# RWKV-7 recurrence of a two-layer decoder trunk: both halves of the inverse in one buffer, the first half ended in the fixed order, gate products and late norms at other places

## The chip, the cores and the metric

The kernel runs on one core of a Trainium2 chip, as one launch. The metric is the device time of that launch in microseconds; the median of three runs stands for the kernel.

## What is computed

The trunk has two layers over 512 positions of width 1024, in float32. Layer 0 is a sparse attention with an indexer, layer 1 is an RWKV-7 time mixing; each is followed by an MLP with squared ReLU. The change touches layer 1 alone:

```python
def step(state, inp):
    r_t, w_t, k_t, v_t, kk_t, b_t = inp
    sa = jnp.einsum('bhvk,bhk->bhv', state, -kk_t)
    state = state * w_t + sa[..., None] * b_t + v_t[..., None] * k_t
    return state, jnp.einsum('bhvk,bhk->bhv', state, r_t)
...
y = (y - mean) * rsqrt(var + LNX_EPS) * lnx_w + lnx_b     # per head of 64
out = (y + bonus) * g                                     # g = sigmoid(xg @ g1) @ g2
return out @ w_o
```

There are 16 heads of 64 columns.

## The kernel before

The 512 steps of the recurrence are done in eight chunks of 64 steps (`NCH` = 8). Within a chunk the dependence of a step on the earlier ones is a unit triangular 64 by 64 system for each head and chunk. Its inverse is built from two 32 by 32 diagonal blocks, inverted on VectorE (`solve`, 30 steps of one multiply, line 1025, and one addition, line 1026), and a corner joined from them by TensorE (`merge1`, line 1120, and `merge2`, line 1132). The inverse comes in two halves: the first is for chunks 0 to 3, the second for chunks 4 to 7. Each half is gathered through DRAM into a tile `tn` of its own, solved in place, copied in a transposed form (`tt`, line 1029, the other half of the same tile), written back to DRAM (`dm` and `dt`, lines 1032 and 1034) and read again into `T11` and `Mt` (lines 1039 and 1042). `tn` and most other large tiles come from one pool of 21 buffers with the tag `b8` (`NB8`); tiles of 512 columns come from one of 17 (tag `t`).

`invert` is a generator. `run(t)` takes steps from it until their estimated cost exceeds `t` nanoseconds; `yield HOLD` ends a call. It is called after each of the eight blocks of the value projection (lines 1205 to 1207) with `RUNW`, and at several places of the recurrence with `RUN1` and `RUN2`.

Up to the value projection a planner sets the order of the instructions from priorities and estimated costs. What follows stands in a `manual_schedule` block: there the five engines' queues take the instructions in the order of the source, while work that was emitted earlier may still be placed between them. In that block each chunk n goes through `step_z` (line 1266, copied by line 1268), `step_u` (line 1274, copied by line 1278), `step_n` (the next state, lines 1292 and 1296), `step_y` (line 1316) and the operands of the next chunk, `opn`/`opl` (lines 1177, 1178, 1172) and `opt` (line 1189). `vcopy` (line 1217) takes the eight value blocks from PSUM into the two tiles `VT`; `vmean` (line 1251) and `vload` (line 1258, GpSimd) prepare them. `g2` makes the gate, eight products of four matmuls (lines 1235 to 1238), of which the last needs a conversion on ScalarE (line 1416). The norm of chunk n's result is `gA` (square, ScalarE), `gB` (sums, VectorE, line 1335), `gC` (root, ScalarE), `gD` (VectorE lines 1347 to 1352, then GpSimd lines 1357 to 1360), and `turn` transposes it (line 1369). `out(f)` makes the operands of the output projection for half f of the positions, one of eight column groups for each `pull` (line 1377, then a split into a high and a low part by line 104 on ScalarE and line 101 or 99). `wom(f, m)` is one output product of 24 matmuls (lines 119 to 121) and a residual addition (line 1393); its weights are converted by ScalarE (line 93) and split by VectorE (line 101) in `wload`, ahead of use.

Of the kernel before, what the change touches and what calls it, by code (L numbers as in the profile page):

```python
# [7 lines left out]
F32 = mybir.dt.float32  # L8
# [757 lines left out]
def rwkv(c, x, ks, gi):  # L766
# [232 lines left out]
    def invert():  # L999
        dn, dm = (c.dram.tile([2, 2, 2, 32, 32, 32], F32, name=v) for v in ("dn", "dm"))  # L1000
        dt = c.dram.tile([2, 2, 32, 32, 32], F32, name="dt")
        mt = [t.rearrange("p q n t -> p (q n) t") for t in Mt]
        for q in range(2):
            qs = slice(16 * q, 16 * q + 16)
            for f in range(2):
                for e in range(2):
                    for b in range(2):
                        r = slice(e * 64 + b * 32, e * 64 + b * 32 + 32)
                        nc.sync.dma_start(dn[f, e, b, qs].rearrange("h i j -> i h j"),
                                          mt[f][r, qs, b * 32:b * 32 + 32])  # L1010
            yield HOLD
        tn = [c.b8("tn", F32, (128, 2, 32, 32)) for _ in range(2)]
        for f in range(2):
            nc.sync.dma_start(tn[f][:, 0].rearrange("p i j -> p (i j)"), dn[f].rearrange("e b h i j -> (e b h) (i j)"))
        yield HOLD
        for f in range(2):
            yield from solve(f, tn[f][:, 0], tn[f][:, 1], mt[f], dm[f], dt[f])

    def solve(f, tn, tt, mt, dm, dt):
        pr = c.t("pr")  # L1020
        for k in range(30, 0, -1):
            nr = 31 - k
            sh = [128, k, nr]
            pv = pr[:, :k * nr].rearrange("p (a b) -> p a b", a=k)
            nc.vector.tensor_mul(pv, tn[:, 0:k, k:k + 1].to_broadcast(sh), tn[:, k:k + 1, k + 1:].to_broadcast(sh))  # L1025
            nc.vector.tensor_add(tn[:, 0:k, k + 1:], tn[:, 0:k, k + 1:], pv)
            yield 2 * (k * nr * 1.04 + 157)
        nc.vector.memset(tn.rearrange("p i j -> p (i j)")[:, 0:1024:33], 1.0)
        nc.vector.tensor_copy(tt, tn.rearrange("p i j -> p j i"))
        stage.append(f)  # L1030
        yield HOLD
        nc.sync.dma_start(dm.rearrange("e b h i j -> (e b h) (i j)"), tn.rearrange("p i j -> p (i j)"))
        for e in range(2):
            nc.sync.dma_start(dt[e].rearrange("h i j -> h (i j)"), tt[e * 64:e * 64 + 32].rearrange("p i j -> p (i j)"))
        yield HOLD
        T11[f] = [c.t("T11").rearrange("p (h j) -> p h j", j=32) for _ in range(2)]
        for e in range(2):
            for g in range(2):
                nc.sync.dma_start(T11[f][g][e * 64:e * 64 + 32], dt[e, g * 16:(g + 1) * 16].rearrange("h i j -> i h j"))
            for b in range(2):  # L1040
                r = slice(e * 64 + b * 32, e * 64 + b * 32 + 32)
                nc.sync.dma_start(mt[r, :, b * 32:b * 32 + 32], dm[e, b].rearrange("h i j -> i h j"))
        yield HOLD

    def run(t):
        while t > 0:
            d = next(inv, None)
            if d is None:
                break
            t -= d  # L1050
# [134 lines left out]
    @c.site("opt")  # L1185
    def opt(n, te=TE):
        pt = c.bank2((128, 8, 2, 64))
        for q in range(8):
            nc.tensor.transpose(pt[:, q].rearrange("p e i -> p (e i)"), sl(KB, n, q).rearrange("p a b -> p (a b)"), ident)
        nc.scalar.activation(BL[n][:, 0, :, 64:128], pt[:, :, 0], AF.Copy)  # L1190
        for i in range(2):
            cp(te[i], BL[n][E2[1 - i], 1, :, 64:128], pt[E2[i], :, 1])
# [38 lines left out]
    @c.site("g2")  # L1231
    def g2(m):
        ms = slice(m * 128, (m + 1) * 128)
        p = c.bank("g")
        nc.tensor.matmul(p, ah[:, ms], sg[0], start=True, stop=False)
        nc.tensor.matmul(p, ah[:, ms], sg[1], start=False, stop=False)
        nc.tensor.matmul(p, al_[:, ms], sg[0], start=False, stop=False)
        nc.tensor.matmul(p, bh[0:96, ms], sg[2][0:96], start=False, stop=True)
        gT[m] = c.t("gT")
        nc.scalar.activation(gT[m], p, AF.Copy, scale=0.5)  # L1240
# [13 lines left out]
    @c.site("vload")  # L1254
    def vload(n):
        SV[n] = sv[:, n % 2]
        for e in range(2):
            nc.gpsimd.tensor_tensor(SV[n][E2[1 - e], e], vt(n)[:, :, e],
                                    vm[E2[n % 2], n // 2, e::2, None].to_broadcast([64, 8, 64]), op=OP.add)

    @c.site("step_z")
    def step_z(n):
        pz = c.bank("g", (128, 8, 64))
        for q in range(8):
            for e in range(2):
                nc.tensor.matmul(pz[E2[e], q], AL[n][:, q, e], SV[n][:, e, q], start=True, stop=True)
        for e in range(2):
            nc.scalar.activation(Zb[E2[e], :, e], pz[E2[e]], AF.Copy)
# [133 lines left out]
    with c.tc.manual_schedule(engines=set(MAN)):  # L1402
        while not stage:
            run(1)
        until(0)
        for i in VL[:3]:
            vcopy(i)
        vmean(0)
        vload(0)
        opn(1, 0)  # L1410
        for i in VL[3:]:
            vcopy(i)
        del ps
        opn(1, 1)
        (ah, al_), (bh, bl) = ((a.rearrange("p a b -> p (a b)") for a in c.wget(0)) for _ in range(2))
        nc.scalar.activation(bh[64:96], bl[64:96].bitcast(F32), AF.Copy)
        g2(0)
        g2(1)
        opt(1, (0, 0))
        g2(2)  # L1420
        g2(3)
        step_z(0)
        for m in range(4, 8):
            g2(m)
        vload(1)
        run(RUN1)
        merge2(0, merge1(0))
        for n in range(NCH - 1):
            more = True
            if n:  # L1430
                step_z(n)
            if n % 2 and more:
                vmean((n + 1) // 2)
            if n == 1:
                lnw = g3(c.t("lnw"))
                nc.sync.dma_start(lnw, c.aps["lnw"])
            if n and more:
                acopy(n + 1)
                opn(n + 1, 0)
                vload(n + 1)  # L1440
            for k in GB.get(n, ()):
                gB(k)
            if n < 3:
                run(RUN2)
            step_u(n)
            if more and n != 3:
                sa[n + 1] = merge1(n + 1)
            for k in GB.get(n, ()):
                gC(k)
            if more:  # L1450
                pn = step_s(n)
                step_n(n, pn)
            py = step_r(n)
            if more:
                sbd(n)
            step_y(n, py)
            for k in GB.get(n, ()):
                gD(k)
            if n < 2:
                run(RUN2)  # L1460
            elif n == 2:
                until(1)
            if n and more:
                opn(n + 1, 1)
            if n == 3:
                sa[4] = merge1(4)
            if more:
                merge2(n + 1, sa[n + 1])
            if n and n < NCH - 2:
                opt(n + 1, (0, 0) if n < 3 else TE)  # L1470
            for k in TU.get(n, ()):
                turn(k)
            for k in GA.get(n, ()):
                gA(k)
            if n == PF1:
                c.wdma()
        n = NCH - 1
        step_z(n)
        c.prefetch(1)
        w0 = out(0)  # L1480
        pull(w0, 4)
        step_u(n)
        gB(5)
        gC(5)
        py = step_r(n)
        step_y(n, py)
        turn(4)
        gA(6)
        gB(6)
        gC(6)  # L1490
        gD(5)
        pull(w0, 4)
        gD(6)
        gA(7)
        gB(7)
        gC(7)
        gD(7, nc.vector)
        xo.extend(c.b8("x") for _ in range(2))
        for i in range(2):
            nc.sync.dma_start(xo[i].rearrange("p a b -> p (a b)"), xs[i])  # L1500
        w1 = out(1)
        for m in range(KC):
            wom(0, m)
            if m in TM:
                turn(TM[m])
            if m > 5:
                pull(w1, 3)
    pull(w1, 8)
    mi = MlpIn(c, gi)
    for m in wo(1):  # L1510
# [7 lines left out]
MAN = (mybir.EngineType.PE, mybir.EngineType.Activation, mybir.EngineType.DVE, mybir.EngineType.SP, mybir.EngineType.Pool)  # L1518
GA = {2: (0,), 3: (1, 2), 4: (3,), 5: (4,), 6: (5,), 7: (6,)}
GB = {3: (0,), 4: (1, 2), 5: (3,), 6: (4,), 7: (5,)}  # L1520
TU = {4: (0,), 5: (1, 2), 6: (3,)}
TM = {1: 5, 3: 6, 5: 7}
PF1 = 5
RQ = 3
VP = (6, 7, 8)
# [1 line left out]
WA = 4  # L1527
LP = 2
OP2 = 1
RUNW = 5000  # L1530
RUN1 = 9000
RUN2 = 2500
XG = 2
# [126 lines left out]
```

## Time and profile before

| | us |
|---|---|
| median of three runs | 1394.31 (1394.28 to 1398.93) |
| the profiled execution, its own time | 1400.04 |
| span of its records | 1398.3 |
| TensorE busy | 1305.3 (93%) |
| VectorE busy | 801.1 (57%) |
| ScalarE busy | 601.8 (43%) |
| GpSimd busy | 176.7 (13%) |

Times within the profile are microseconds from the start of the span. In a timeline row the first number is the start, the second the duration of the instruction or of the merged run of them, then engine, line, operation, output and inputs, and in brackets how long the engine had stood idle and what released it. TensorE's busy time counts a matmul until its modelled end, so a busy stretch is not one at the full clock; the granted clock is given beside it as a share of 2.4 GHz.

### The profile page before, as it was taken

The page shows a single profiled execution, that of the slowest core. Times are in us where ns is not written, and L with a number is a line of the kernel's source. Part 1 is how long each engine was busy: PE and PEld are TensorE (multiplying, and loading weights), DVE is VectorE, ACT ScalarE, POOL GpSimd, SP SyncE. Part 2 cuts the span into 40 slices and gives each one's busy share as a digit, 9 for nine tenths or more (in the row PEclk, how much of TensorE's full clock was granted, in tenths as well). Part 3 has the DMA queues.
Part 4 walks back from the last instruction along what each step waited for, and adds up shares of the span by engine and source line. Part 5 has one row for each costly group of instructions (what it writes and reads, how often), then busy time and mean ns, then how long its engine had stood idle before and what let it go on. Part 6 is the DMA issues. An engine that isn't in the chain of part 4 may idle for free.

```text
span 1398.3 us, 20066 instructions
## 1 busy us (share of the span) xinstructions
PE 1305.3 (93%) x8197; PEld 1070.6 (77%) x8197; DVE 801.1 (57%) x1407; ACT 601.8 (43%) x1024; POOL 176.7 (13%) x176
## 2 busy tenths in 40 slices
PE   8989899999999999999998968884999999999997
PEld 6766566888888888898677856763888888888887
DVE  5689974454421545259889886566565433244523
ACT  5535693343311434139765425653444331134421
POOL 0385750000000000000000011354020000000000
PEclk9999999999999999999999988996999999999999
DMA  7100023221323215232203421414432132321401
GB/s 282 61 30 31 1 75 109 97 90 61 120 95 117 90 60 181 91 106 76 90 31 87 140 53 40 78 26 165 133 109 82 69 121 90 121 90 62 170 10 61
DMA packets 63932, 125.95 MB, mean 90 GB/s; under 512 B 32608, under 2 KB 35296, under 8 KB 63072
## 3 DMA queue, kind: packets, MB, share of 16 engines
q1 hardware_dynamic: 61600, 122.44, 26.6%
q10 hardware_dynamic: 2240, 2.24, 0.5%
q8 instruction: 64, 1.05, 0.3%
q14 instruction: 28, 0.23, 0.1%
HBM read 115.74 MB, written 6.82 MB: 88 GB/s over the span
## 4 chain that ended last, share of the span: by engine, by line
PE 80%; DVE 12%; ACT 4%; issue 2%; POOL 1%; DMA 0%; DVEq 0%; ACTq 0%; SPq 0%; POOLq 0%
PE g L121 19%; PE g L119 19%; PE g L120 19%; PE g L628 2%; DVE rot L411 1%; PE d L613 1%; DVE w L101 1%; DVE acc L497 1%; DVE L L587 1%; DVE m L495 1%; PE g L993 1%; DVE pr L1025 1%; PE g L1274 1%; PE g L1292 1%; PE d L386 1%
## 5 line engine op out<-in xcount | busy, mean ns | idle before, releaser
L101 DVE TENSOR_TENSOR w<-wraw,w 128x1024 fp32r<-128x1024 f32 x189 | 229.7, 1239 | 116.4 <-ACT w L93 116.2
L93 ACT ACTIVATE w<-wraw 128x1024 fp32r<-128x1024 f32 x198 | 201.0, 1048 | 135.3 <-DMA wraw<-in_wblk 103.6
L119 PE MATMUL g<-sh,w 128*128 128x512 f32 (+1 forms) x608 | 216.5, 356 | 0.0
L120 PE MATMUL g<-sl,w 128*128 128x512 f32 (+1 forms) x608 | 216.2, 356 | 0.0
L121 PE MATMUL g<-sh,w 128*128 128x512 f32 (+1 forms) x608 | 216.2, 356 | 0.0
L120 PE MATMUL g<-al,w 128*128 128x512 f32 x512 | 199.3, 389 | 0.6 <-DVE al L257 0.6
L119 PE MATMUL g<-ah,w 128*128 128x512 f32 x512 | 199.7, 390 | 0.0
L121 PE MATMUL g<-ah,w 128*128 128x512 f32 x512 | 199.4, 389 | 0.3 <-DVE w L101 0.3
L273 ACT ACTIVATE sh<-r 128x512 fp32r<-128x512 f32 x64 | 40.4, 631 | 227.0 <-DVE r L271 227.0
L119 PEld LDWEIGHTS g<-sh,w 128*128 128x128 f32 x608 | 114.9, 189 | 16.4
L120 PEld LDWEIGHTS g<-sl,w 128*128 128x128 f32 x608 | 114.9, 189 | 16.2
L121 PEld LDWEIGHTS g<-sh,w 128*128 128x128 f32 x608 | 114.9, 189 | 16.2
L120 PEld LDWEIGHTS g<-al,w 128*128 128x128 f32 x512 | 96.1, 188 | 20.8 <-DVE al L257 1.0
L121 PEld LDWEIGHTS g<-ah,w 128*128 128x128 f32 x512 | 96.1, 188 | 20.5 <-DVE w L101 0.7
L119 PEld LDWEIGHTS g<-ah,w 128*128 128x128 f32 x512 | 96.1, 188 | 19.9
L271 DVE SCALAR_TENSOR_TENSOR r<-g,rstd 128x512 f32<-128x512 f32 x64 | 44.1, 691 | 95.5 <-PE g L121 84.6
L275 DVE TENSOR_TENSOR sl<-q,sh 128x512 fp32r<-128x512 f32 x64 | 44.4, 693 | 75.0 <-ACT q L274 75.0
L295 DVE TENSOR_TENSOR x<-g,x 128x512 f32<-128x512 f32 x26 | 18.0, 692 | 107.0 <-PE g L121 107.0
L179 ACT ACTIVATE sq<-x 128x256 f32<-128x256 f32 (+1 forms) x56 | 26.7, 500 | 110.7 <-DVE x L295 57.4
L922 POOL MEMSET seg<- 128x512 f32 x1 | 0.5, 527 | 487.2 <-DVE xl L101 487.2
L119 PE MATMUL g<-oh,w 128*128 128x256 f32 x128 | 39.8, 315 | 8.8 <-ACT w L93 4.9
L121 PE MATMUL g<-oh,w 128*128 128x256 f32 x128 | 38.8, 307 | 7.4 <-DVE w L101 7.4
(316 smaller groups left out, 2485.8 us busy)
## 6 DMA issues: line engine op xcount, KB each, us to landing
wraw<-in_wblk SPq DMA_DIRECT2D x98, 1024.0 KB, 4.9
wraw<-in_wblk SPq DMA_DIRECT2D x5, 512.0 KB, 6.1
x<-in_xT SPq DMA_DIRECT2D x8, 256.0 KB, 5.3
x<-in_xT SPq DMA_DIRECT2D x2, 1024.0 KB, 6.9
xs<-x SPq DMA_DIRECT2D x2, 1024.0 KB, 4.9
abd<-AR SPq DMA_DIRECT2D x64, 32.0 KB, 1.9
x<-xs SPq DMA_DIRECT2D x2, 1024.0 KB, 6.5
dn<-Mt SPq DMA_DIRECT2D x16, 64.0 KB, 3.4
```

What stands on the lines that cost most here:

```text
L93: s.wsp = s.nc.scalar.activation(hi, r, AF.Copy)
L101: s.nc.vector.tensor_sub(out, a, b)
L119: s.nc.tensor.matmul(p, whi[:, kc, :], ahi, start=first and kc == 0, stop=False)
L120: s.nc.tensor.matmul(p, whi[:, kc, :], alo, start=False, stop=False)
L121: s.nc.tensor.matmul(p, wlo[:, kc, :], ahi, start=False, stop=last and kc == KC - 1)
L179: nc.scalar.activation(sq, xk, AF.Square)
L271: nc.vector.scalar_tensor_tensor(r, p, 0.0, rstd, op0=OP.max, op1=OP.mult)
L273: nc.scalar.activation(hi, r, AF.Square)
L275: nc.vector.tensor_sub(lo, q, hi.bitcast(F32))
L295: nc.vector.tensor_add(xm, p, xm)
L386: nc.tensor.matmul(ps[m], wl, hi, start=False, stop=k == KC - 1)
L628: nc.tensor.matmul(po[HF[e]], v[sc // 2][:, j:j + 64], st8[tb, pr, e][:, sc], start=sc == 0, stop=sc == tb)
```

## The change

Both halves share one tile `tn` of the `b8` pool; the transposed copy goes into two tiles of the `t` pool, and is written to DRAM by four transfers instead of two. `RUNW` goes from 5000 to 2200, so that 25 of the first half's 30 steps are emitted within the value projection and the last five in the `manual_schedule` block, where they stand in the fixed order ahead of `vmean(0)`. In that block the gate products, the first `step_z`, `opt(1)` and the two merges come in another order. `turn(3)` moves to the start of chunk 6. The eight `pull`s of `out(0)` are spread around the last chunk's `step_z` and `step_u`; two weight blocks are prepared there instead of one. The norms of chunks 5, 6 and 7 move from before the output products to between the first three of them, and the turns with them.

```diff
-        tn = [c.b8("tn", F32, (128, 2, 32, 32)) for _ in range(2)]
+        tn = c.b8("tn", F32, (128, 2, 32, 32))
...
-            yield from solve(f, tn[f][:, 0], tn[f][:, 1], mt[f], dm[f], dt[f])
+            yield from solve(f, tn[:, f], mt[f], dm[f], dt[f])
...
-        nc.vector.tensor_copy(tt, tn.rearrange("p i j -> p j i"))
+        tt = [c.t("tt").rearrange("p (i j) -> p i j", j=32) for _ in range(2)]
+        for g in range(2):
+            nc.vector.tensor_copy(tt[g], tn.rearrange("p i j -> p j i")[:, 16 * g:16 * g + 16])
...
-            nc.sync.dma_start(dt[e].rearrange("h i j -> h (i j)"), tt[e * 64:e * 64 + 32].rearrange("p i j -> p (i j)"))
+            for g in range(2):
+                nc.sync.dma_start(dt[e, :, 16 * g:16 * g + 16], tt[g][e * 64:e * 64 + 32])
...
         g2(1)
-        opt(1, (0, 0))
+        step_z(0)
         g2(2)
         g2(3)
-        step_z(0)
-        for m in range(4, 8):
-            g2(m)
+        opt(1, (0, 0))
         vload(1)
+        g2(4)
+        g2(5)
         run(RUN1)
-        merge2(0, merge1(0))
+        sa[0] = merge1(0)
+        g2(6)
+        merge2(0, sa[0])
+        g2(7)
...
+            if n == 6:
+                turn(3)
...
+        w0 = out(0)
+        pull(w0, 4)
         n = NCH - 1
         step_z(n)
+        pull(w0, 2)
+        step_u(n)
         c.prefetch(1)
-        w0 = out(0)
-        pull(w0, 4)
-        step_u(n)
-        gB(5)
-        gC(5)
+        pull(w0, 2)
+        c.prefetch(2)
         py = step_r(n)
         step_y(n, py)
         turn(4)
-        gA(6)
-        gB(6)
-        gC(6)
-        gD(5)
-        pull(w0, 4)
-        gD(6)
-        gA(7)
-        gB(7)
-        gC(7)
-        gD(7, nc.vector)
...
         for m in range(KC):
             wom(0, m)
+            if m < 3:
+                if m:
+                    gA(m + 5)
+                gB(m + 5)
+                gC(m + 5)
+                gD(m + 5, nc.vector if m == 2 else nc.gpsimd)
             if m in TM:
                 turn(TM[m])
             if m > 5:
-                pull(w1, 3)
+                pull(w1, 4)
...
-TU = {4: (0,), 5: (1, 2), 6: (3,)}
-TM = {1: 5, 3: 6, 5: 7}
+TU = {4: (0,), 5: (1, 2)}
+TM = {2: 5, 4: 6, 5: 7}
...
-RUNW = 5000
+RUNW = 2200
```

## Rows read from the trace of the kernel before

**Rows 1.** Busy times by stretch: us, then each engine, granted clock, DMA share, GB/s.
```profile
core 0: us, PE busy (x) PEld busy (x) DVE busy (x) ACT busy (x) POOL busy (x), PEclk, DMA share, GB/s
...
819.50:848.70 29.20, 16.91 (x200) 12.97 (x200) 22.52 (x60) 12.74 (x23) 3.63 (x4) 0.77 0.38 73
...
956.00:982.00 26.00, 13.10 (x56) 11.22 (x54) 19.12 (x32) 6.58 (x13) 12.06 (x10) 0.57 0.12 40
982.00:1000.30 18.30, 18.30 (x155) 18.30 (x154) 9.53 (x15) 7.36 (x10) 0.00 (x0) 1.00 0.51 173
```
**Rows 2.** Waits of TensorE from 750 to 1015: us in total, times, longest.
```profile
PE g L121 <- DVE w L101: 7.4, 3, 5.7
PE d L1177 <- DVE pr L1025: 6.3, 1, 6.3
...
PE g L1238 <- ACT w L1416: 4.5, 1, 4.5
```
**Rows 3.** Waits of ScalarE from 800 to 1010.
```profile
ACT VT L1217 <- DMA dt<-tn: 13.5, 1, 13.5
```
**Rows 4.** Timeline from the first half's step 22 to the last reload issue.
```profile
812.96 0.36 DVE L1026 TENSOR_TENSOR tn<-tn,pr 128x198 f32<-128x198 f32 x1
...
817.24 1.22 DVE L1251 TENSOR_REDUCE vm<-VT 128x16 f32<-128x1024 f32 x1 [3.92 <-ACT VT L1217]
...
819.10 0.39 PE L1207 MATMUL g<-w,xl 128*128 128x512 f32 x1
...
819.14 1.06 DVE L1025 TENSOR_TENSOR pr<-tn 128x168 f32<-128x168 f32 x1
...
827.55 1.05 DVE L1029 COPY tn<-tn 128x1024 f32<-128x1024 f32 x1
...
831.21 0.60 ACT L1217 ACTIVATE VT<-d 128x512 f32<-128x512 f32 x1 [13.51 <-DMA dt<-tn]
...
834.72 0.56 SPq L1042 DMA_DIRECT2D Mt<-dm  x1
```
**Rows 5.** Landing of the reloads of line 1042.
```profile
DMA to landing us min/median/max: 3.3/3.6/4.2
```
**Rows 6.** Timeline of the second half's first steps, and merge to `step_u(0)`.
```profile
830.30 0.18 DVE L1025 TENSOR_TENSOR pr<-tn 128x30 f32<-128x30 f32 x1
...
835.32 0.37 DVE L1025 TENSOR_TENSOR pr<-tn 128x198 f32<-128x198 f32 x1
...
845.62 0.69 PE L1120 MATMUL g<-T,Mt 32*32 32x32 f32 x32
...
848.72 1.97 PE L1274 MATMUL g<-bd,Mt 128*64 128x128 f32 x16 [0.85 <-ACT Mt L1112]
```
**Rows 7.** Timeline from the last `step_u` to the first output half's end.
```profile
952.01 1.58 ACT L1278 ACTIVATE sv<-g 64x256 f32<-64x256 f32 x4
...
956.11 0.56 PE L119 MATMUL g<-oh,w 128*128 128x256 f32 x1
...
957.64 0.69 DVE L1335 TENSOR_REDUCE gst<-sq 128x8 f32<-128x512 f32 x1 [4.82 <-ACT sq L1329]
...
959.27 0.69 DVE L1352 TENSOR_TENSOR y<-y,gst 128x512 f32<-128x512 f32 x1
...
970.08 0.58 PE L119 MATMUL g<-oh,w 128*128 128x256 f32 x1 [2.87 <-ACT w L93]
...
975.27 2.35 DVE L101 TENSOR_TENSOR w<-wraw,w 128x1024 fp32r<-128x1024 f32 x2
...
977.54 0.42 DVE L1393 TENSOR_TENSOR x<-g,x 128x256 f32<-128x256 f32 x1
...
981.40 0.80 PE L1369 MATMUL g<-ident,y 128*128 128x128 f32 x4
...
1000.06 0.28 PE L121 MATMUL g<-oh,w 128*128 128x256 f32 x1
```
**Rows 8.** Instructions of GpSimd from 810 to 980, grouped by line.
```profile
L1359 POOL TENSOR_TENSOR y<-y,lnw 128x512 f32<-128x512 f32 x7 | 9.0, 1288 | 31.1 <-ACT y L1321 13.0 <-DVE y L1352 9.6 <-DVE gst L1347 8.4
```

More of the change, by code (lines that the diff above doesn't have):

```diff
@@ L1011, in invert, with solve @@
             yield HOLD
-        tn = [c.b8("tn", F32, (128, 2, 32, 32)) for _ in range(2)]
+        tn = c.b8("tn", F32, (128, 2, 32, 32))
         for f in range(2):
-            nc.sync.dma_start(tn[f][:, 0].rearrange("p i j -> p (i j)"), dn[f].rearrange("e b h i j -> (e b h) (i j)"))
+            nc.sync.dma_start(tn[:, f].rearrange("p i j -> p (i j)"), dn[f].rearrange("e b h i j -> (e b h) (i j)"))
         yield HOLD
         for f in range(2):
-            yield from solve(f, tn[f][:, 0], tn[f][:, 1], mt[f], dm[f], dt[f])
-    def solve(f, tn, tt, mt, dm, dt):
+            yield from solve(f, tn[:, f], mt[f], dm[f], dt[f])
+    def solve(f, tn, mt, dm, dt):
         pr = c.t("pr")
```

## The prediction

> **What bounds the kernel now.** The page comes first: TensorE is busy for 93% of the span, so only stretches where it isn't can give time back. I went through the value projection, the recurrence and the output projection by stretches. Three of them carry the argument [rows 1]. From 819.5, where the value projection ends, to 848.7, where `step_u(0)` starts, TensorE is busy for 16.9 of 29.2 us at a mean granted clock of 0.77. From 956 to 982 it is busy for 13.1 of 26 us at 0.57, close to the lower level (1.2 GHz). From 982 to 1000.3, in the same output products, it is busy all the time at the full clock. The list of TensorE's waits names the causes [rows 2]: 6.3 us for a PSUM buffer of `opl`, 4.5 us for the gate weights' conversion, 5.7 us at once for a weight split on VectorE. These add up to 16.5 us; the slower clock comes on top.
>
> What stands behind the first two of these waits is seen in ScalarE's own list [rows 3]: the fourth of the eight value copies stood 13.5 us for the write-back `dt<-tn`. A copy needs nothing from the inverse; it waited for a buffer. `VT` is two `b8` tiles, and the second had to take the buffer of the first half's `tn`, which is free only when its transposed part has left. That came late because the first half's solve ended late [rows 4]: 22 of its 30 steps were over at 813.3, then VectorE stood for `vmean`, and the last eight were strewn among other work until the transposed copy at 827.55. So `VT` went on at 831.2.
>
> The second stretch is a matter of order. The second output product starts at 970.1 [rows 7], but its weight split is queued on VectorE behind the norm of chunk 7, which itself waits for GpSimd; it runs at 975.3. The first product's last operands stand behind the norm of chunk 5 in the same way.
>
> **First part: shared `tn`, the first half ended in order.** I count `b8` buffers at the fourth value copy from the source: AR 4, KB 4, Mt 2, the gate's sigmoid, abd, BL 2, VT 2, sv, bd, two gate weights, the last value weight: 21, and `tn`. With two `tn` that is 23 for 21 buffers: one tile can follow the value weight, free after the last value matmul at 819.5 [rows 4], the other must wait for `tn`, as the trace shows. With one `tn` it is 22, and only the first of these waits is left. I take 819.6 for the fourth copy; five copies at a pace of 0.5 end at 822.1, and the conversion of the gate weights (1.05) at about 823.2. TensorE then has no 6.3 us wait, and 1 to 2 us instead of 4.5 for the conversion.
>
> The solve: the second half's first eight sizes, 30 to 198 columns, took 830.30 to 835.32 [rows 6]. The first half's last eight have sizes 30 to 184, and 198 is only the end mark of that stretch, so its 5.0 us hold for them. From 813.3 they end at 818.3; memset and two copies of half size (1.05 together [rows 4]) end at 819.5 instead of 828.6. `vmean` starts then, 2.3 us later than now; `vload(0)` behind it on GpSimd still ends before 823.5, when `step_z(0)` wants it. From the copy's end to the landing of the last reload now takes 10.3 us: last issue ended at 835.28, landing 3.6 [rows 4, 5]. Two more write-back issues on SP's queue add at most 0.56 each. So the reload lands at 819.5 + 10.3 + 1.1 = 830.9. `merge1(0)` has been moved ahead of two gate products, so it meets that landing; `merge1` to `step_u(0)` took 3.1 us [rows 6], with the two products now in its gaps. `step_u(0)` starts at 834.0 against 848.7: 14.7 us. TensorE's own work is no tighter bound: 16.9 us at 0.77 is 13.0 at full clock, from 819.5 to 832.5.
>
> What is late next: 18 steps of the second half run on VectorE from about 824; before, they were done in 14 us, ten before the next state's product asked for VectorE. Now they end at about 838, when that product comes. Each us more would go to the chain, so I take 14. The bounds: up to 16 if the landing is no limit (832.5), 8 if the planner holds the 25 steps back to the pace of the value blocks. In that case four steps of the eighth block, 2.8 us, and the last five, 2.8, run after 819.5, the copy ends at 826.3, and everything here is 6.8 late. The `tt` tiles cost nothing: by my count of the `t` pool the second half brings it to exactly 17. If one is missing, a square on ScalarE waits for the write-back, 2 to 3 us. Chunks 1 to 6 otherwise shift as a block; `turn(3)` moves into a gap of TensorE.
>
> **Second part: `out(0)` spread, norms 5 to 7 among the products.** Four `pull`s now stand on ScalarE ahead of `step_z(7)`'s copies, which delays them by about 3 us, but the copies of `step_u` no longer wait behind them: I have those over at 952.3 against 953.6 now [rows 7]. The last two pulls wait behind a weight split until about 957.6. So the first product starts at about 956.2, as now, but goes through to 959.2; the norms are no longer ahead of it. The second follows at once, since its weights were prepared by the second `prefetch`.
>
> From there VectorE sets the pace up to the sixth product, whose split stands behind norm 7. Its list from 960.2: four splits at 1.18, three additions at 0.42, three norms at 2.3 (957.64 to 959.96), and two more passes of 0.69 for norm 7 [rows 7]: 4.7 + 1.3 + 6.9 + 1.4 = 14.3, so 974.5. That is the end without collisions. GpSimd works on the same norms meanwhile: ten instructions at 1.29 or less, 12.9 us [rows 8]. When both engines read two tiles, VectorE is held up: a step of 168 columns took 1.06 beside `vload`, one of 198 alone 0.37 [rows 4, 6]. If each held VectorE for its whole length, the sixth split would end at 987.4. Sums over one tile and reads of PSUM aren't hit, so I take a third: 978.8. Then three products at 2.88 (six products and two turns of 0.56 from 981.96 to 1000.34 [rows 7]) and one turn follow: 978.8 + 8.6 + 0.6 = 988.0. Now it is 1000.3: 12.3 us, taken as 12. The bound above is TensorE's own work, 956.2 + 8 × 2.88 + 3 × 0.56 = 980.9, a gain of 19; the one below is full exclusion, 996.6, a gain of 4.
>
> PSUM is no limit: four `g` buffers, and an addition frees one before the third product after it. The weight transfers wait for buffers freed by earlier products, so they move up with them. What follows 1000.3 keeps its order.
>
> **Sum.** 14 + 12 = 26 us. Against the profiled execution, 1400.0 - 26 = 1374.0; that execution is 5.7 us above the median of the runs, so for the median 1394.3 - 26 = 1368.
>
> **Rivals.**
> A (0.60): as worked out, 1368; its own range, from 11 to 16 and 9 to 17, is 1361 to 1374.
> B (0.15): GpSimd's norms hold the weight splits to the full; the second part gives 4, the sum 18, the time 1376. For it speaks the 168-column step, stretched to just the length of a `vload` instruction; against it, that only part of VectorE's list reads two tiles from SBUF. The Trainium skill (SBUF — State Buffer, section "SBUF: two separate sides") states this as a rule: VectorE and GpSimd share a port pair by an exclusive lock, and the loser waits for the whole instruction. By that rule the moved norms cost their full length wherever they meet, and the time is B's; the trace agrees for the steps beside `vload` (1.06 us), and no run so far shows it for the new order.
> C (0.08): the planner paces the solve; the first part gives 8, the sum 20, the time 1374.
> D (0.07): the change doesn't do what it says. `VT` still waits for a buffer, held by something outside my count; the first stretch keeps its 29 us, only the second gains: 1382.
> E (0.04), slower: the products starve behind fixed-order VectorE work. The two that now stand beside the norms take about 11.2 us each (970.1 to 981.4 [rows 7]). If all eight did, the half would end at 956.2 + 90 + 1.7 = 1048, 47 us later than now; less 14, that is 33 slower, 1427. It decides from (1000.3 - 956.2 - 1.7 + 14 + 7) / 8 = 7.9 us a product on. Against it: only three have a norm beside them; with three at 11.2 the half ends at 1006, and the kernel still gains 8.
> F (0.06): both stretches keep their length under other waits, within 0.5% (7 us), about what a measurement here can tell from no change.
>
> The range 1360 to 1383 holds A, C, most of B and D. Faster by over 0.5%: A to D less the slow ends of B and D, 0.89; within: 0.07; slower: 0.04.
>
> **What would show it.** Right: no wait of line 1217 for `dt<-tn`; the first transposed copy near 819; `step_u(0)` some 14 us after the value projection's end; no wait above 3 us of TensorE in the first output half, which lasts about 32 us instead of 44. Wrong: `VT` waiting for another release, `merge1(0)` waiting long for `T11`, VectorE's splits stretched to 2 us and more, or a granted clock near 0.5 through the products.

## The result, and the profile after

The changed kernel takes 1375.0 us (median of four runs, 1373.16 to 1376.3) against 1396.16 for the kernel before on the same chip: a ratio of 0.9846, with a 95% interval of 0.9821 to 0.9871. That is faster, 21 us by the medians; 1368 was forecast, with a range of 1360 to 1383. The profiled execution took 1375.85 us with a span of 1374.0, that is 24.3 us less than the span of before. The changed kernel's line numbers are two higher than those of before from line 1029 on and three higher from line 1034 on; rows below carry its own.

The same stretches as in [rows 1], busy times by engine, then the granted clock of TensorE, DMA share and GB/s:

```profile
core 0: us, PE busy (x) PEld busy (x) DVE busy (x) ACT busy (x) POOL busy (x), PEclk, DMA share, GB/s
818.00:834.00 16.00, 13.74 (x203) 10.55 (x202) 13.68 (x39) 12.15 (x22) 4.18 (x4) 1.00 0.69 129
834.00:925.40 91.40, 76.20 (x1761) 63.42 (x1760) 60.88 (x139) 55.25 (x115) 33.72 (x31) 0.93 0.23 47
925.40:937.50 12.10, 6.30 (x105) 6.10 (x100) 5.80 (x14) 7.61 (x16) 4.82 (x5) 0.72 0.77 282
...
937.50:975.60 38.10, 30.00 (x208) 28.99 (x207) 29.18 (x46) 13.69 (x22) 15.24 (x11) 0.87 0.44 157
```

The first row runs from the last value matmul to `step_u(0)`: 16.0 us instead of 29.2. The second ends at `step_z(7)`, the third at the first output product, the fourth at the end of the first output half: 38.1 us instead of 44.2. Set against before:

| stretch | before | after | gain | forecast |
|---|---|---|---|---|
| start to the last value matmul | 819.5 | 818.0 | 1.5 | 0 |
| to `step_u(0)` | 29.2 | 16.0 | 13.2 | 14.7, taken as 14 |
| to `step_z(7)` | 94.2 | 91.4 | 2.8 | 0 |
| to the first output product | 13.2 | 12.1 | 1.1 | 0 |
| to the end of the first half | 44.2 | 38.1 | 6.1 | 12.3, taken as 12 |
| to the end | 398.0 | 398.4 | -0.4 | 0 |

The 1.5 us of the first line can't be laid to the change: in the profiles of the eight experiments below that leave everything ahead of that end as in the changed kernel (`e1`, `e5` to `e8`, `v1` to `v3`) it lies between 817.3 and 821.6. The new timeline of the first stretch, with the rows that answer to [rows 4] and [rows 6] (start, duration, engine, line, operation):

```profile
817.05 1.18 DVE L1031 COPY tt<-tn 128x512 f32<-128x512 f32 x2
...
818.04 0.60 ACT L1220 ACTIVATE VT<-d 128x512 f32<-128x512 f32 x1 [1.82 <-PE g L1210]
...
824.67 1.09 SPq L1045 DMA_DIRECT2D Mt<-dm  x2
...
833.97 1.09 PE L1277 MATMUL g<-bd,Mt 128*64 128x128 f32 x16
```

The solve is over before the value projection is; the fourth value copy goes on at once, and waits for a value matmul, no longer for a write-back. TensorE's waits from 750 to 1000 (in total, times, longest), to be read beside [rows 2]:

```profile
PE g L1277 <- ACT bd L1271: 14.6, 6, 5.8
PE g L121 <- DVE w L101: 5.8, 4, 3.1
...
PE g L1372 <- POOL y L1363: 2.8, 1, 2.8
PE d L1180 <- DVE BL L1175: 2.2, 1, 2.2
```

The wait of 6.3 us for a buffer of `opl` has shrunk to 2.2, that for the gate weights' conversion is gone, and the longest wait for a weight split is 3.1 instead of 5.7 (four of them add up to 5.8). Two are new: `step_u(7)` waits 5.8 us for `step_z(7)`'s copies (behind the four pulls), and the turn of chunk 5 waits 2.8 us for the norm's last GpSimd instruction.

### The profile page after: what moved, and what is told of

The parts are those of the page before. It is cut to its first block, busy times and chain, and to the rows that moved or that the text cites. A ratio compares the mean times of both kernels' runs of the same rounds, so it can differ in the third digit from the quotient of the medians.

```text
span 1374.0 us, 20074 instructions
## 1 busy us (share of the span) xinstructions
PE 1295.1 (94%) x8197; PEld 1064.6 (77%) x8197; DVE 796.1 (58%) x1409; ACT 601.9 (44%) x1024; POOL 180.4 (13%) x176
## 4 chain that ended last, share of the span: by engine, by line
PE 77%; DVE 14%; issue 4%; ACT 4%; POOL 1%; DMA 0%; ACTq 0%; DVEq 0%; POOLq 0%
PE g L121 19%; PE g L119 19%; PE g L120 19%; DVE w L101 2%; PE g L628 2%; DVE rot L411 1%; PE d L613 1%; DVE pr L1025 1%; DVE tn L1026 1%; DVE acc L497 1%; DVE L L587 1%; DVE m L495 1%; PE g L1277 1%; PE g L993 1%; PE d L384 1%
## 5 line engine op out<-in xcount | busy, mean ns | idle before, releaser
L121 PE MATMUL g<-oh,w 128*128 128x256 f32 x128 | 39.0, 309 | 9.2 <-DVE w L101 7.7
L597 ACT ACTIVATE L<-L,st 128x256 f32<-128x256 f32 (+3 forms) x64 | 35.1, 553 | 14.1 <-DVE st L595 14.0
```

The lines of the kernel that those rows point to most:

```text
L121: s.nc.tensor.matmul(p, wlo[:, kc, :], ahi, start=False, stop=last and kc == KC - 1)
L597: nc.scalar.activation(L[g][:, :n], L[g][:, :n], AF.Exp, bias=nmx[:, g:g + 1], scale=0.125, accum_out=sm[:, g:g + 1])
```

## The experiments

Times are medians; each ratio is to the kernel before, timed alongside. The changed kernel's is 0.9846.

**The two parts by themselves.** `e1` puts the tail of before back into the changed kernel, `e2` puts the new tail into the kernel before (the tail is everything of the diff from `turn(3)` on, with `TU` and `TM`).

> The changed kernel with the tail (pulls, prefetch, turn of chunk 3, norms 5 to 7) put back as before; the first part stays. My theory (two independent parts, the first worth some 13 us): step_u(0) stands about 16 us after the last value matmul as in the changed kernel, against 29.2 before; the output products keep their 44 us from the first product's start to the half's end; time 1383 us, ratio to before near 0.991. Rival (the parts lean on each other, the first's gain is eaten before the output products without the second): ratio above 0.996.

> The kernel before with the tail of the changed kernel; two tn tiles, RUNW 5000 and the old gate order stay. My theory: step_u(0) stays 29 us after the last value matmul, the stretch from step_u(0) to the end of the first output half shrinks by 10 to 11 us; time 1386 us, ratio near 0.9925. Rival (the tail gains only because the earlier chain is denser and the clock higher): ratio above 0.997.

`e1`: 1383.5 us, 0.9901 (0.9882 to 0.9920). `e2`: 1389.9 us, 0.9946 (0.9933 to 0.9958), where 1386 and 0.9925 had been expected. The shares, 0.0099 and 0.0054, add up to the whole change's 0.0154 within their intervals: no dependence between the parts shows, and the first is the larger. In `e1` the first half of the products keeps its length (44.4 us); in `e2` `step_u(0)` stays at 29.8 us after the value projection. From there to the end of the first output half `e2` is 14.2 us shorter than before, more than the 10 to 11 expected, but its profiled execution was the fastest of five.

**What in the first part it was.** Three edits of the changed kernel: a tile for each half again, `RUNW` back at 5000, and both.

```diff
e3, e9
-        tn = c.b8("tn", F32, (128, 2, 32, 32))
+        tn = [c.b8("tn", F32, (128, 2, 32, 32)) for _ in range(2)]
...
-            yield from solve(f, tn[:, f], mt[f], dm[f], dt[f])
+            yield from solve(f, tn[f][:, 0], mt[f], dm[f], dt[f])
e4, e9
-RUNW = 2200
+RUNW = 5000
```

> The changed kernel with a tn tile for each half again (the transposed copies stay in the t pool), so that one more b8 buffer is held. My theory: the solve's end sets the release now, so the fourth value copy waits only for the write-back dm, about 3 us (from 818 to 821 on the changed kernel's scale), and the kernel loses 0 to 3 us, since the reload sets merge1(0). Rival (the buffer is the whole of the first part): the copies wait some 10 us or more and the kernel loses about 10 to 13 us.

> The changed kernel with RUNW 5000: all 30 steps of the first half are emitted inside the value projection and the planner may strew the last of them among later work. My theory (order of the solve is the larger term): the transposed copy starts some 8 us later, merge1(0) waits for the reload, step_u(0) comes about 7 us later, the kernel loses 6 to 8 us. Rival (the buffer is the whole): value copies still go on at once, the loss is 0 to 2 us.

> The changed kernel with two tn tiles and with RUNW 5000: buffer and solve order are both undone, the new order of the gate products and the whole second part stay. Alone, the two cost step_u(0) 2.0 us (two tiles) and 6.4 us (RUNW). Theory of one chain (late solve, late write-back, late release: each half of the edit covers for the other): together they cost more than the sum of 8.4, step_u(0) at 27 to 29 us after the last value matmul, time near that of the run with the second part only. Theory of a sum (independent terms, the rest of the 13 us is the order of the gate products): step_u(0) at 24 to 25.

| kernel | time, ratio (interval) | transposed copy | fourth value copy | `step_u(0)` | granted clock |
|---|---|---|---|---|---|
| changed | 1375.0, 0.9846 (0.9821 to 0.9871) | -1.0 | 0.0 | 16.0 | 1.00 |
| `e3` two tiles | 1376.8, 0.9849 (0.9832 to 0.9865) | -1.1 | 3.3 | 18.0 | 0.91 |
| `e4` RUNW 5000 | 1379.9, 0.9873 (0.9860 to 0.9886) | 7.4 | 0.0 | 22.4 | 0.85 |
| `e9` both | 1386.1, 0.9928 (0.9914 to 0.9941) | 8.1 | 10.9 | 27.8 | 0.75 |
| before | | 8.1 | 11.7 | 29.2 | 0.77 |

The last four columns are from each kernel's profile: us from the last value matmul, and the mean granted clock from there to `step_u(0)`. With the solve ended early, undoing the shared tile costs 2.0 us at `step_u(0)`, and nothing that the time can show. Part of the 2.0 is the clock: `e1`, which has the changed kernel's instructions up to there, took 17.3 at 0.90. Undoing the order costs 6.4 (5.1 against `e1`). Both undone cost 11.9, more than the sum of 8.4. Put in alone, each is worth more: from `e9` the shared tile gives 5.4 us (to 22.4) and the order 9.8 (to 18.0). It is one chain, in which a late solve makes a late write-back and a late release, and each half of the edit covers for part of the other. (In `e9` the fourth copy goes on 2.9 us after `dm` is issued; the wait list names a gate product there, from which the copy takes nothing.) `e4`'s wait list says why order matters even where the copies go on at once:

```profile
PE d L1180 <- DVE pr L1025: 6.1, 1, 6.1
```

This is the 6.3 us wait of before, with `VT` no longer waiting: TensorE's PSUM buffer is freed by masks on VectorE, and the planner had strewn the solve's steps ahead of them and among them. About half of this wait is a collision: four of these steps stand beside `vload(0)` on GpSimd and are about 3 us longer together than in the changed kernel, where they are over before `vload(0)` starts. One of them in `e4`, and the same step in the changed kernel:

```profile
817.96 1.05 DVE L1025 TENSOR_TENSOR pr<-tn 128x150 f32<-128x150 f32 x1
```
```profile
813.49 0.32 DVE L1025 TENSOR_TENSOR pr<-tn 128x150 f32<-128x150 f32 x1
```

In the time the order shows as 3.8 us by the ratios, with intervals that overlap. `merge1(0)` was expected to wait for the reload in `e4`; no such wait is in its list. In `e3` ScalarE's list shows the release that is left, now the write-back `dm`:

```profile
ACT VT L1220 <- DMA dm<-tn: 5.1, 1, 5.1
```

**The order of the gate products.** `e5` restores it alone:

```diff
-        step_z(0)
+        opt(1, (0, 0))
         g2(2)
         g2(3)
-        opt(1, (0, 0))
+        step_z(0)
+        for m in range(4, 8):
+            g2(m)
         vload(1)
-        g2(4)
-        g2(5)
         run(RUN1)
-        sa[0] = merge1(0)
-        g2(6)
-        merge2(0, sa[0])
-        g2(7)
+        merge2(0, merge1(0))
```

> The changed kernel with the gate products, step_z(0), opt(1) and the merges in the order of before; everything else stays. My theory (with the solve ended early the order of the gate products only fills gaps): merge1(0) comes after all eight products, about 2 us later, and nothing is left to fill the gaps of the merges, 1 to 1.5 us more; step_u(0) 3 to 4 us later after the last value matmul (19 to 20 against 16), kernel slower by 2 to 4 us. Rival (the order of the gate products is a large part of the first stretch): 6 us or more.

1378.7 us, 0.9860 (0.9844 to 0.9875); `step_u(0)` at 17.2 us, at a granted clock of 1.00 as in the changed kernel. So the order of the gate products is worth 1.2 us there; I had expected 3 to 4.

**What in the second part it was.** `e6` puts the norms of chunks 5 to 7 behind `turn(4)`, ahead of all output products; `e7` puts pulls and prefetch back as before; `e8` moves the norms' GpSimd instructions to VectorE.

```diff
e6
+        for m in range(3):
+            if m:
+                gA(m + 5)
+            gB(m + 5)
+            gC(m + 5)
+            gD(m + 5, nc.vector if m == 2 else nc.gpsimd)
         xo.extend(c.b8("x") for _ in range(2))
...
             wom(0, m)
-            if m < 3:
...
e7
-        w0 = out(0)
-        pull(w0, 4)
         n = NCH - 1
         step_z(n)
-        pull(w0, 2)
-        step_u(n)
         c.prefetch(1)
-        pull(w0, 2)
-        c.prefetch(2)
+        w0 = out(0)
+        pull(w0, 4)
+        step_u(n)
         py = step_r(n)
         step_y(n, py)
         turn(4)
+        pull(w0, 4)
e8
-            nc.gpsimd.tensor_tensor(bv[E2[b]].rearrange("p (a e i) -> p a e i", a=4, e=2), v4[:, :, b],
+            (eng if n > 4 else nc.gpsimd).tensor_tensor(bv[E2[b]].rearrange("p (a e i) -> p a e i", a=4, e=2), v4[:, :, b],
...
-                gD(m + 5, nc.vector if m == 2 else nc.gpsimd)
+                gD(m + 5, nc.vector)
```

> The changed kernel with the norms of chunks 5 to 7 ahead of the output products again (behind turn(4)); pulls, prefetch, turns and the first part stay. My theory (the order of the norms against the weight splits is the larger term of the second part): the third block's split stands behind all three norms, some 14 to 18 us of VectorE; the first two products run, then TensorE stands for about 10 us; the kernel loses 5 to 8 us. Rival (the pulls and the early second block are the whole): loss 0 to 2 us.

> The changed kernel with the pulls of out(0) and the prefetch as before (four behind step_z(7) with one weight block, four behind turn(4)); norms among the products, the turns and the first part stay. My theory: the copies of step_z(7) no longer wait for the pulls (4 us earlier), but the last four column groups come later, so that the first product ends some 3 us later than in the changed kernel: loss 0 to 4 us. Rival (the pulls are the larger term): loss 6 us or more.

> The changed kernel with the GpSimd instructions of the norms of chunks 5 to 7 (bonus products, scale, addition) on VectorE: no two engines meet there any more, but VectorE's list grows by ten instructions of about 0.7, some 7 us. Theory order (splits late because of what is queued before them): first output half longer by 4 to 7 us. Theory collision (splits and norms late because GpSimd holds the other engine up): first output half the same or up to 3 us shorter.

`e6`: 1382.7 us, 0.9879 (0.9861 to 0.9897): 4.6 us lost by the ratios, and TensorE stands 8.2 us (10 were expected) for a weight conversion queued behind the norms' roots on ScalarE:

```profile
PE g L119 <- ACT w L93: 8.2, 1, 8.2
```

`e7`: 1380.3 us, 0.9874 (0.9860 to 0.9889), 3.9 us lost by the ratios, where 0 to 4 were expected; its profiled execution, 1377.9 us, was the fastest of four. `step_u(7)` starts 2.8 us after `step_z(7)` instead of 7.1, but the first product comes 13.3 us after `step_z(7)` instead of 12.1. By their times the two can't be told apart, and the intervals of both overlap the changed kernel's. By place, `step_z(7)` to the end of the first half takes 55.6 us in `e6`, 52.8 in `e7` and 50.3 in the changed kernel, with granted clocks in the half of 0.84, 0.83 and 0.87. So the order of the norms is the larger term by one profile of each, no more. `e8`: 1376.0 us, 0.9846 (0.9823 to 0.9869): no difference in time. The first output half is 36.3 us long in its profile against 38.1, as theory collision had it, but at a granted clock of 0.91 against 0.87, so the length alone doesn't decide. VectorE has ten instructions more and no one to meet; its sixth weight split, which frees the sixth product, is here, against the changed kernel's below it:

```profile
965.52 1.22 DVE L101 TENSOR_TENSOR w<-wraw,w 128x1024 fp32r<-128x1024 f32 x1
```
```profile
962.60 1.22 DVE L101 TENSOR_TENSOR w<-wraw,w 128x1024 fp32r<-128x1024 f32 x1
```

From the first product to that split's end are 27.2 us in `e8` and 26.3 in the changed kernel. The ten instructions take 6.9 us in `e8`, so meeting GpSimd cost about 6.9 - (27.2 - 26.3) = 6.0 us in the changed kernel; the VectorE instructions that last longer there than in `e8` make 5.9. Neither theory alone holds: collision and queue cost about the same.

**Versions meant to be faster.** `v1` queues the weight splits two blocks further ahead, `v2` also lets `step_z(7)`'s copies go ahead of the pulls, `v3` also puts `opn(1, 1)` behind two gate products.

```diff
v1
-        c.gemm(p, c.wget(WA if f else 2), o[f])
+        c.gemm(p, c.wget(4), o[f])
...
-            if m > 5:
-                pull(w1, 4)
+            if m == 6:
+                pull(w1, 8)
...
-TM = {2: 5, 4: 6, 5: 7}
+TM = {4: 5, 5: 6, 6: 7}
v2, besides
         w0 = out(0)
-        pull(w0, 4)
         n = NCH - 1
         step_z(n)
-        pull(w0, 2)
+        pull(w0, 4)
         step_u(n)
         c.prefetch(1)
-        pull(w0, 2)
+        pull(w0, 4)
v3, besides
-        opn(1, 1)
         (ah, al_), (bh, bl) = ...
...
         g2(1)
+        opn(1, 1)
         step_z(0)
```

> The changed kernel with the weight splits of the first output half queued two blocks further ahead (wget(4) instead of wget(2)), so that three stand on VectorE ahead of the norm of chunk 5; the turns of chunks 5, 6, 7 one product later, and the eight pulls of out(1) at once behind the last turn. Theory order: TensorE waits for no split in the first five products, the half then waits only for norm 7's turn, 2 to 4 us; the half ends 3 to 5 us earlier, time 1370 to 1372. Theory collision (the norms, not the splits, set the pace): the last turn is as late as in the changed kernel, 31 us after the first product, and the time the same within 1 us.

> The same, and the first four pulls of out(0) stand behind step_z(7)'s copies instead of ahead of them. My theory: step_u(7) starts about 3 us after step_z(7) instead of 7, its copies end 2 to 3 us earlier, the first product starts 1 to 2 us earlier: 1 to 2 us less than the run before. Rival (the last column groups set the first product whatever the copies do): no difference.

> The same as the run before, and the second half of chunk 1's operand products stands behind the first two gate products on TensorE, so that it doesn't wait there for the masks to free a PSUM buffer. My theory: the 2.2 us wait is filled, step_u(0) comes 14 us after the last value matmul instead of 16, time 2 us less. Rival (the reload sets merge1(0)): merge1(0) then waits for the reload, gain below 1 us.

`v1`: 1376.5 us, 0.9845 (0.9818 to 0.9873). `v2`: 1373.1, 0.9831 (0.9808 to 0.9855). `v3`: 1375.5, 0.9849 (0.9828 to 0.9869). None is told apart from the changed kernel, and so none of the gains expected is shown. In `v1` the long waits for a split are gone (the longest is 1.5 us), but two others stand in their place:

```profile
PE g L1372 <- DVE x L1396: 3.2, 1, 3.2
PE g L119 <- DVE x L1396: 3.1, 1, 3.1
```

The products run ahead until the four PSUM buffers are full, because the additions that free them are queued behind the same norms. In `v2` `step_u(7)` starts 2.8 us after `step_z(7)`, as expected, and the first product 10.5 us after it instead of 12.1; the half's end, 49.1 us after `step_z(7)`, is about where it was in `v1` (49.5). In `v3` `step_u(0)` stays at 17.3 us, as in `v1`, where 14 were expected: TensorE now waits 1.8 us for the gate weights' conversion, which I hadn't counted there.

## Why the prediction was right, and which terms were off

**The mechanism of the first part held, and its size nearly.** Against the value projection's end, `step_u(0)` came 13.2 us earlier (forecast 14.7, taken as 14) and the transposed copy 9 us. That `step_u(0)` stands at 833.97, where 834.0 was forecast, is luck: 1.5 us of that lie ahead of the value projection's end. Two steps were off. I put TensorE's first two waits down to the buffer. For the 4.5 us of the conversion that is right: the wait is 3.7 in `e9` and gone in `e4`. For the 6.3 us it isn't: `e4`, whose copies wait for no buffer, keeps 6.1 of them, which is VectorE's order. And I let the reload set `merge1(0)`. It doesn't: nothing in the trace waits for it there. The last reload's issue ends at 825.8 and lands 3.2 to 3.9 us later, before `merge1(0)` starts at 830.2. What sets `merge1(0)` is TensorE's own work, and the 2.2 us wait for the masks, for which the forecast had no term. The 10 us of slack that the second half's solve had was used up as foreseen, all but 0.3: ahead of the product for the next state VectorE stood 10.3 us for TensorE before, and 0.3 now.

```profile
854.23 1.41 DVE L1296 TENSOR_TENSOR sv<-g,pc 64x512 f32<-64x512 f32 x2 [10.33 <-PE g L1292]
```
```profile
837.88 1.41 DVE L1299 TENSOR_TENSOR sv<-g,pc 64x512 f32<-64x512 f32 x2 [0.29 <-PE g L1295]
```

**The step that failed is the length of the first output half.** It was forecast as 31.8 us (956.2 to 988.0) and took 38.1. The sixth weight split's end was forecast 22.6 us after the first product and came after 26.3. Three terms of the list make up the difference. Collisions cost 6.0 us by `e8`, where a third of the bound, 4.3, had been taken. The second product's split, 1.2 us, was taken as done ahead of the list; it stands in it, and TensorE waited for it:

```profile
943.70 0.38 PE L121 MATMUL g<-oh,w 128*128 128x256 f32 x1 [1.47 <-DVE w L101]
```

And a norm takes 2.7 us (945.89 to 948.58 for chunk 5), not 2.3: the rows from which 2.3 was read hold the sum of chunk 6 and the rest of chunk 5, without the wait for a root between them; three norms make 1.1. Two splits of 2.04 and 1.98 us are one of the signs of being wrong that the forecast named. A split beside a GpSimd instruction took 1.98 us instead of 1.23:

```profile
943.66 1.98 DVE L101 TENSOR_TENSOR w<-wraw,w 128x1024 fp32r<-128x1024 f32 x1
```

The Trainium skill (SBUF — State Buffer, section "SBUF: two separate sides") has this as an exclusive lock, and the trace agrees for such instructions; the list as a whole paid about half of the full exclusion of rival B. From the sixth split to the half's end took 11.8 us instead of 9.2, and that is the clock, 0.73 there; in `e4`, whose tail is the same instructions, this piece took 9.0 at 1.00. The changed kernel, then `e4`:

```profile
963.80:975.60 11.80, 11.73 (x75) 11.73 (x76) 6.35 (x12) 2.38 (x4) 0.00 (x0) 0.73 0.42 152
```
```profile
969.30:978.30 9.00, 8.96 (x75) 8.97 (x76) 6.31 (x11) 2.38 (x4) 0.00 (x0) 1.00 0.51 196
```

The whole half, in the same order:

```profile
937.50:952.20 14.70, 9.70 (x75) 8.89 (x73) 11.98 (x20) 6.79 (x12) 7.11 (x6) 1.00 0.60 216
952.20:968.70 16.50, 13.40 (x80) 13.20 (x81) 13.80 (x20) 4.51 (x7) 8.13 (x6) 0.73 0.33 111
968.70:975.60 6.90, 6.90 (x55) 6.90 (x54) 3.40 (x7) 2.38 (x4) 0.00 (x0) 0.90 0.34 141
```
```profile
943.95:957.70 13.75, 9.38 (x75) 8.76 (x73) 11.01 (x19) 6.82 (x12) 7.15 (x6) 0.99 0.61 205
957.70:972.10 14.40, 11.25 (x81) 11.04 (x82) 13.68 (x19) 4.48 (x7) 8.09 (x6) 0.89 0.32 116
972.10:978.30 6.20, 6.20 (x55) 6.20 (x54) 3.51 (x8) 2.38 (x4) 0.00 (x0) 1.00 0.47 170
```

Both stand 2.8 us for the turn of chunk 5 and 3.1 for the sixth split. The changed kernel then runs at 0.73 of the full clock, `e4` at 0.89, and the half takes 38.1 us in the one and 34.4 in the other. Of these 3.7 us, 1.0 is no loss: `e4`'s first product starts that much later after `step_z(7)` (13.1 against 12.1 us), and has no wait for its own split, where the changed kernel has one of 0.5.

**What offset it was not in the sum.** The chain from `step_u(0)` to `step_z(7)` got 2.8 us shorter. Of this, 2.0 lie in chunk 6 alone, where `turn(3)` was moved, an edit that I had costed at nothing. From `step_u(6)` to `step_z(7)` before, and in `e2`:

```profile
933.70:942.90 9.20, 9.19 (x200) 7.45 (x200) 4.57 (x12) 4.77 (x12) 1.65 (x2) 0.81 0.12 23
```
```profile
931.20:938.50 7.30, 7.26 (x198) 6.17 (x198) 4.02 (x10) 4.93 (x11) 1.06 (x2) 1.00 0.08 16
```

The stretch is 9.2 us at a granted clock of 0.81 where `turn(3)` stands at its end (before and `e1`), and 7.3 at 1.00 in the kernels with the turn ahead of `step_u(6)`. That the transposes in the gap keep the clock up is the likeliest reading; no run moved the turn alone, so it is not shown apart from the rest of the tail. The last 0.8 us are not attributed; kernels alike in the whole chain differ there by up to 1.5 us.

So the total is nearer than its terms. The two terms of the sum were 6.7 us too large together (0.8 and 5.9), and 5.0 came from stretches that were not in it; this makes 24.3 of the 26 us in the profiles, and 21 by the medians. That the errors partly cancel is luck.

Rivals: it was A's mechanism with its second term too large, and the time lies 1 us outside A's own range (1361 to 1374), inside the whole one. B's price for the second part (4, sum 18, 1376) lies close to the time, but its full exclusion isn't what happened. C, D and F fell: the solve was over 1 us before the value projection, `VT` waited for nothing from the inverse, and both stretches shrank. E fell with the 38.1 us, 4.8 a product.

## What to carry to other kernels

When a copy waits for a buffer, ask what made its release late, and what else stands behind that: here the order of 30 small steps on VectorE was worth more than the buffer, whether undone alone (6.4 against 2.0 us) or put in alone (9.8 against 5.4), and undoing either left part of the gain in place. When slow work is moved in among work that another engine waits for, price its collisions from the nearest rows, and the clock that TensorE may lose behind a new wait. Taking one wait away ahead of a full queue mostly shows the next: splits, then the additions that free PSUM.

## What the runs showed of the hardware that I hadn't expected

The same instructions behind the same waits run at different granted clocks from one profile to the next, and this is several us. Besides the output half (38.1 us at 0.87 and 34.4 at 0.95 overall), the stretch from the last value matmul to `step_u(0)`, with its one wait of 2.2 us, took 16.0 us at 1.00 in the changed kernel, `e6`, `e7` and `e8`, and 17.3 at 0.90 in `e1`, `v1` and `v2`, which have the same instructions there. What decides between the two is not shown. Executions of one kernel differ in the same way: `e6` took 1377.8 us at a mean granted clock of 0.979 and 1383.0 at 0.975. Row by row, the changed kernel's is shown above; `e1`'s reads:

```profile
820.40:837.80 17.40, 15.17 (x203) 11.71 (x202) 14.13 (x41) 12.15 (x22) 4.17 (x4) 0.90 0.63 119
```

So differences of 1 to 4 us between single profiles of these kernels are no evidence of an edit's worth by themselves; comparisons by place need the clock beside them.
